# Gate and up projections of three FFNs as two by two block products: seven for eight

## The chip, the cores and the metric

The kernel runs on one core of one Trainium2 chip. The metric is device microseconds of one launch, the median of several runs. Profiles come from one profiled execution, which has a time of its own.

## The reference

A trunk of two decoder layers over 512 positions of width 1024, in float32. Each layer is a half FFN, a mixer, and a second half FFN, each added to x:

```
def swiglu_half(x, g, w_gate, w_up, w_down):
    h = rms_norm(x, g)
    return (jax.nn.silu(h @ w_gate) * (h @ w_up)) @ w_down
# x = x + 0.5 * swiglu_half(...)   four times: FFN 1 to 4; d_ff = 2816
```

Layer 0 mixes by MLA and dilated window attention, layer 1 by window attention with sinks and sparse attention. So the order is FFN 1, mixer 0, FFN 2, FFN 3, mixer 1, FFN 4.

## The kernel before, in words

x lies transposed on the chip: 8 tiles `x[d]` of 128 (width) x 512 (positions). TensorE multiplies in fp32r, and every operand is split in two: hi, its value cast to fp32r (ScalarE), and lo, the rest (VectorE, `tensor_tensor` subtract). A product is three matmuls: hi x hi, lo x hi, hi x lo (`TERMS`). `split` (L165 to L172) makes the pair; for weights it is one cast `whi<-raw` and one subtraction `wlo<-raw,whi` per tile of up to 1024 columns, three raw buffers deep.

An FFN (`ffn`, L262) runs in two halves of 11 features (a feature is 128 of the 2816 columns). For a feature, gate (bank `pg`) and up (`pu`) take 8 width tiles x 3 terms = 24 matmuls of 512 columns each, every one with its own weight load. `gated` (L295) scales both by the norm `rb` on VectorE, takes the silu on ScalarE, multiplies, and splits the result in ah and al. Then the half's down product follows: 8 blocks `py`, 33 matmuls each, and `x<-py,x` (L289).

The norm is put off: matmuls read x times the gain (`norm_tile`, L176: xh, xl of a d as soon as x[d] is done), and the sum of squares goes beside it (a square on ScalarE, an add on GpSimd, L195). `norm_wide` turns it into `rb` by a matmul with ones and by 9 VectorE operations of 512 columns (`rsqrt`). It is called in the first feature.

The Tile scheduler orders each engine's instructions by priority, which is the order of the code unless `high_priority` lifts them; each engine's queue is then served in order, and semaphores join them. Weight loads are DMAs on the SP queue. Buffers have tags with fixed counts (`UNITS`, `BANKS`): an allocation waits until the tile that had the buffer is done with.

## Time and profile before

| what | us |
|---|---|
| runs (3) | 2001.82, 2003.4, 2003.5; median 2003.4 |
| the profiled execution, its own time | 2003.07 |
| its span, first to last instruction | 2001.3 |
| TensorE busy | 1975.6 |
| VectorE, ScalarE, GpSimd busy | 1011.0, 754.2, 157.6 |

A row of the trace has the line, the engine, the operation, out<-in by the program's names, shapes and count; times are in us unless marked ns. PEld is the weight load, POOL is GpSimd, DVE VectorE, ACT ScalarE. A matmul's duration is longer than the step to the next, as they are pipelined: the step is read from two starts.

### The profile page before, as it was taken

To read this page: it belongs to the slowest core of one execution; us is meant where nothing else is said; L and a number is where in the kernel's file an instruction comes from. 1 tells how busy PE (TensorE), PEld (TensorE's weight loads), DVE (VectorE), ACT (ScalarE), POOL (GpSimd) and SP (SyncE) were. 2 spreads that over 40 slices of the span, in tenths; PEclk is the share of its full clock that TensorE was granted. 3 is DMA by queue.
4 is the path that set the end of the run, shared out by engine and by line. 5 is a ranking of instruction groups with operands and counts; after the bars stand their busy time and mean duration, and the time that the engine had idled before them with its cause. 6 is when DMAs were issued, how large, how long until landed. Compare 5 with 4: busy or idle time off the path is not lost.

```text
span 2001.3 us, 24703 instructions
## 1 busy us (share of the span) xinstructions
PE 1975.6 (99%) x9559; PEld 1628.5 (81%) x9559; DVE 1011.0 (51%) x1956; ACT 754.2 (38%) x1298; POOL 157.6 (8%) x219
## 2 busy tenths in 40 slices
PE   8999999999999999999999999999999999999999
PEld 6888888987967888888888888889987678888887
DVE  5443444477555644344454434445667765433442
ACT  4222333346555332232333223234267853322321
POOL 6100000112112000000100000001011220000000
PEclk9999999999999999999999999999999999999999
DMA  6523223421122222322332232244201132232323
GB/s 193 181 85 114 86 103 118 149 73 53 48 61 65 104 95 91 109 89 92 94 108 93 90 111 95 92 141 162 75 25 59 48 111 95 90 93 102 105 88 102
DMA packets 72854, 194.55 MB, mean 97 GB/s; under 512 B 9540, under 2 KB 16216, under 8 KB 72736
## 3 DMA queue, kind: packets, MB, share of 16 engines
q1 hardware_dynamic: 70752, 186.90, 28.3%
q0 software_dynamic: 1984, 6.06, 1.2%
q8 instruction: 75, 1.23, 0.2%
q14 instruction: 43, 0.35, 0.1%
HBM read 186.59 MB, written 12.35 MB: 99 GB/s over the span
## 4 chain that ended last, share of the span: by engine, by line
PE 95%; DVE 2%; ACT 1%; issue 1%; DMA 0%; POOL 0%; SPq 0%; DVEq 0%; ACTq 0%; POOLq 0%
PE py L162 27%; PE pg L162 24%; PE pu L162 24%; PE pz L404 10%; PE s L456 3%; PE po L497 2%; PE pt L434 2%; PE pqt L434 1%; ACT e L451 1%; PE pq L162 0%; PE ph L931 0%; DMA x<-in_xT 0%; ACT th L443 0%; DVE e L450 0%; PE pk L162 0%
## 5 line engine op out<-in xcount | busy, mean ns | idle before, releaser
L169 DVE TENSOR_TENSOR wlo<-raw,whi 128x1024 fp32r<-128x1024 f32 (+4 forms) x386 | 397.3, 1029 | 518.4 <-ACT whi L168 512.5
L168 ACT CAST whi<-raw 128x1024 fp32r<-128x1024 f32 (+4 forms) x386 | 345.4, 895 | 731.8 <-PE pu L162 298.7
L162 PE MATMUL pg<-xh,whi 128*128 128x512 f32 x704 | 276.0, 392 | 6.7 <-ACT xh L171 6.7
L162 PE MATMUL pg<-xl,whi 128*128 128x512 f32 x704 | 275.5, 391 | 1.9 <-DVE xl L172 1.9
L162 PE MATMUL pg<-xh,wlo 128*128 128x512 f32 x704 | 275.6, 391 | 0.0
L162 PE MATMUL pu<-xh,wlo 128*128 128x512 f32 x704 | 274.3, 390 | 0.0
L162 PE MATMUL pu<-xh,whi 128*128 128x512 f32 x704 | 274.0, 389 | 0.0
L162 PE MATMUL pu<-xl,whi 128*128 128x512 f32 x704 | 273.9, 389 | 0.0
L162 PE MATMUL py<-ah,whi 128*128 128x512 f32 x704 | 273.9, 389 | 0.0
L162 PE MATMUL py<-ah,wlo 128*128 128x512 f32 x704 | 273.9, 389 | 0.0
L162 PE MATMUL py<-al,whi 128*128 128x512 f32 x704 | 273.9, 389 | 0.0
L301 ACT ACTIVATE tg<-tg 128x512 f32<-128x512 f32 x88 | 55.6, 632 | 323.1 <-DVE tg L300 323.1
L162 PEld LDWEIGHTS pg<-xh,whi 128*128 128x128 f32 x704 | 132.5, 188 | 35.9 <-ACT xh L171 8.0
L162 PEld LDWEIGHTS pg<-xh,wlo 128*128 128x128 f32 x704 | 132.7, 188 | 35.1 <-DVE wlo L169 1.2
L162 PEld LDWEIGHTS pg<-xl,whi 128*128 128x128 f32 x704 | 132.5, 188 | 29.3 <-DVE xl L172 4.5
L162 PEld LDWEIGHTS pu<-xl,whi 128*128 128x128 f32 x704 | 132.1, 188 | 27.7 <-issue 0.2
L162 PEld LDWEIGHTS pu<-xh,wlo 128*128 128x128 f32 x704 | 132.1, 188 | 27.6 <-issue 0.2
L162 PEld LDWEIGHTS py<-ah,whi 128*128 128x128 f32 x704 | 132.1, 188 | 27.6
L162 PEld LDWEIGHTS py<-al,whi 128*128 128x128 f32 x704 | 132.1, 188 | 27.6
L162 PEld LDWEIGHTS pu<-xh,whi 128*128 128x128 f32 x704 | 132.2, 188 | 27.4
L162 PEld LDWEIGHTS py<-ah,wlo 128*128 128x128 f32 x704 | 132.1, 188 | 27.1
L300 DVE TENSOR_TENSOR tg<-pg,rb 128x512 f32<-128x512 f32 x88 | 60.8, 691 | 179.4 <-PE pg L162 179.3
(291 smaller groups left out, 2592.7 us busy)
## 6 DMA issues: line engine op xcount, KB each, us to landing
raw<-in_gu SPq DMA_DIRECT2D x174, 512.0 KB, 3.5
raw<-in_dn SPq DMA_DIRECT2D x64, 384.0 KB, 3.0
raw<-in_dn SPq DMA_DIRECT2D x64, 320.0 KB, 2.8
raw<-in_cd SPq DMA_DIRECT2D x14, 512.0 KB, 3.4
raw<-in_abqk SPq DMA_DIRECT2D x12, 512.0 KB, 3.8
xd<-x SPq DMA_DIRECT2D x16, 256.0 KB, 2.0
x<-xd SPq DMA_DIRECT2D x16, 256.0 KB, 4.0
raw<-in_abv SPq DMA_DIRECT2D x6, 512.0 KB, 3.6
```

The costliest lines, as they stand in the source:

```text
L162: self.nc.tensor.matmul(p, lhsT=w, rhs=x, start=n == 0, stop=n == len(terms) - 1)
L168: nc.scalar.copy(hi, src)
L169: nc.vector.tensor_tensor(lo, src, hi.bitcast(F32), OP.subtract)
L300: nc.vector.tensor_tensor(tg, ps[0], rb, OP.mult)
L301: nc.scalar.activation(tg, tg, AF.Silu)
L404: self.nc.tensor.matmul(ps[i], lhsT=sel(self.xg[k][b], i), rhs=wt[a][:, k - ks[0]], start=first, stop=k == KT - 1 and b == 1, skip_group_c ...
L434: self.turn = self.nc.tensor.transpose(p[:o[0], o[1]:o[1] + 128], s, self.identr if s.dtype == F32R else self.ident)
L451: nc.scalar.activation(s, s, AF.Exp, bias=st, scale=-1.0, accum_out=ss)
L456: self.nc.tensor.matmul(d, lhsT=a[:, q * 128:(q + 1) * 128], rhs=b[:, cols[0]:cols[1]], start=start and n == 0, stop=n == len(terms) - 1, ...
L497: self.nc.tensor.matmul(o, lhsT=v, rhs=t, start=first and k == 0, stop=last and k == len(heads[0]) - 1, skip_group_check=True)
```

## The change

FFN 2 to 4 use `ffn_combined`. Per feature, the 2 x 2 blocks of the weights are gate and up by lower and upper half of the width (a11, a12 gate; a21, a22 up); those of x are the width halves by the halves of the positions (256 columns). Seven products of 4 width tiles x 3 terms replace eight:

- `combine` loads a feature's weights as two raw tiles and makes four sums of 128 x 512 on GpSimd; `part` splits them (ScalarE, VectorE): 11 with s3, s1 with s2, 12 with 22, and s4.
- `norm_pair` makes the sums of x for tiles p and p+4 on GpSimd and VectorE, and splits them. The down and output products before such an FFN run their blocks in the order `PAIRED`.
- The products go to halves of three banks p, q, r. ScalarE copies p, q and r's first products out, VectorE and GpSimd put gate and up together (uu, tg, tu), and the scaling by rb is on GpSimd (tu) and VectorE (tg).
- `then` ties each of these instructions behind the last one on its engine: ACT, DVE and POOL run them in the order written. The splits for feature f+1 and the sums for f+2 stand between the steps of f, and the silu and splitting of f-1 too.
- Down runs after thirds of 8, 7 and 7 features instead of halves of 11.
- Buffers: raw four for three; z 17 and 4 pairs for 25; e and b one less. In mixer 0 the steps a20 and a11 change places. FFN 1 stays as it was, but that its last down product runs its blocks in the order `PAIRED`.

```diff
@@ -34,12 +34,16 @@
         "F3": (256, (0, 8), 1, 0, 127, 1),
         "F4": (512, (8, 16), 1, 0, 511, 1)}
-UNITS = {"x": 8, "xm": 16, "z": 25, "o": 8, "qk": 4, "e": 9, "t": 6, "h": 2, "b": 5}
+UNITS = {"x": 8, "xm": 16, "zz": 4, "z": 17, "o": 8, "qk": 4, "e": 8, "t": 6, "h": 2, "b": 4}
 BANKS = {"s": 2, "t": 2, "o": 1, "q": 1, "f": 2}
+RAWS = 4
 TERMS = ((0, 0), (1, 0), (0, 1))
-
-ORDER0 = """a10 !p0 a00 !h0 !h1 !p1 a20 a01 a11 a12 a02 !h2 s10 !s00 a21 s02 !h3 !s11 !s12 s01 !o0 !o1"""
+THIRDS = (0, 8, 15, 22)
+PAIRED = (0, 4, 1, 5, 2, 6, 3, 7)
+ORDER0 = """a10 !p0 a00 !h0 !h1 !p1 a11 a01 a20 a12 a02 !h2 s10 !s00 a21 s02 !h3 !s11 !s12 s01 !o0 !o1"""
 SCALE_F, SCALE_D, SCALE_T, SCALE_W = "vgvg", "gavv", "ggav", "avgv"
 SQUARE = "ggva"
...
-        return self.pu.tile([128, 512], dt, name=name, tag=tag, bufs=UNITS[tag])
+        return self.pu.tile([128, 1024 if tag == "zz" else 512], dt, name=name, tag=tag, bufs=UNITS[tag])
+    def doubled(self, name):
+        t = self.u("zz", name)
+        return [t[:, 0:512], t[:, 512:1024]]
     def ps(self, tag, name, dt=F32):
         return self.pp.tile([128, 512], dt, name=name, tag=tag, bufs=BANKS[tag])
...
@@ -121,7 +130,7 @@
     def load(self, src):
         a, b = src.shape[1:]
-        raw = self.pw.tile([128, a * b], F32, name="raw", tag="raw", bufs=3)
+        raw = self.pw.tile([128, a * b], F32, name="raw", tag="raw", bufs=RAWS)
         self.nc.sync.dma_start(raw, src.rearrange("p a b -> p (a b)"))
         return raw
...
@@ -180,9 +189,43 @@
             nc.sync.dma_start(self.xd[d], x)
         hi, lo = self.u("xm", "xh", F32R), self.u("xm", "xl", F32R)
         self.split(x, hi, lo, self.gn[:, j, d:d + 1])
-        self.xg.append((hi, lo))
+        self.xg.setdefault(d, (hi, lo))
         if squares:
             self.squares(d)
+    def norm_next(self, j, d, paired, spill=False):
+        if not paired:
+            self.norm_tile(j, d, spill)
+            return
+        self.squares(d)
+        if d >= 4:
+            self.norm_pair(j, d - 4)
+    def norm_pair(self, j, p):
+        nc = self.nc
+        n = 14 * p // 2
+        tags = (["xm"] * 16 + ["z"] * 12)[n:n + 7]
+        g = [self.u("t", "xg") for _ in range(2)]
+        for t, d in zip(g, (p, p + 4)):
+            nc.scalar.activation(t, self.x[d], AF.Copy, scale=self.gn[:, j, d:d + 1])
+        lo, hi = slice(0, 256), slice(256, 512)
+        c = [self.u("t", "xc") for _ in range(2)]
+        nc.gpsimd.tensor_tensor(c[0][:, lo], g[0][:, hi], g[0][:, lo], OP.subtract)
+        nc.vector.tensor_tensor(c[0][:, hi], g[1][:, hi], c[0][:, lo], OP.subtract)
+        nc.gpsimd.tensor_tensor(c[1][:, lo], g[1][:, hi], g[0][:, hi], OP.subtract)
+        nc.vector.tensor_tensor(c[1][:, hi], g[1][:, lo], c[0][:, hi], OP.subtract)
+        b = {}
+        for m, (t, names) in enumerate(((g[1], ("21", "22")), (c[0], ("t1", "t2")), (c[1], ("t3", "t4")))):
+            h, l = self.u(tags[2 * m], "xh", F32R), self.u(tags[2 * m + 1], "xl", F32R)
+            self.split(t, h, l)
+            for name, half in zip(names, (lo, hi)):
+                b[name] = h[:, half], l[:, half]
+        t = self.u(tags[6], "xh", F32R)
+        b["11"] = t[:, lo], t[:, hi]
+        self.split(g[0][:, lo], *b["11"])
+        self.xg.append(b)
     def squares(self, d):
         nc, x = self.nc, self.x[d]
...
@@ -263,8 +306,8 @@
         nc = self.nc
         gu, dn = self.A["gu"][li], self.A["dn"][li]
         xg = self.xg
-        self.xg = []
-        atags = ["o"] * 8 + ["e"] * 9 + ["b"] * 3 + ["qk"] * 2
+        self.xg = {}
+        atags = ["o"] * 8 + ["e"] * 8 + ["b"] * 3 + ["qk"] * 3
         for half in range(2):
             a = []
             for f in range(half * HF, (half + 1) * HF):
...
@@ -282,14 +325,144 @@
                 self.gated(a, ps, rb, atags)
                 if setup and f > 1:
                     next(setup, None)
-            for d in range(KT):
-                w = self.weights(dn[half, d], 6)
+            for d in PAIRED if half else range(KT):
+                w = self.weights(dn[d][:, half * HF:half * HF + HF], 6)
                 p = self.ps("f", "py")
                 self.mm3(p, [(w[f][i], a[f][j]) for f in range(HF) for i, j in TERMS])
                 nc.vector.scalar_tensor_tensor(self.x[d], p, 0.5, self.x[d], OP.mult, OP.add)
                 if half:
                     if nj is not None:
-                        self.norm_tile(nj, d, spill)
+                        self.norm_next(nj, d, False, spill)
+                    if out is not None:
+                        nc.sync.dma_start(out[:, d, :], self.x[d])
+    def then(self, eng, op, *args):
+        e = {"a": self.nc.scalar, "v": self.nc.vector, "g": self.nc.gpsimd}[eng]
+        with self.tc.issue_after(self.last[eng].ins) if eng in self.last else nullcontext():
+            self.last[eng] = getattr(e, op)(*args)
+    def parts_then(self, src, hi, lo):
+        self.then("a", "copy", hi, src)
+        self.then("v", "tensor_tensor", lo, src, hi.bitcast(F32), OP.subtract)
+    def combine(self, src):
+        r = [self.load(src[:, 4 * n:4 * n + 4]).rearrange("p (a b) -> p a b", a=4) for n in range(2)]
+        g, u = slice(0, 128), slice(128, 256)
+        a11, a21, a12, a22 = r[0][:, :, g], r[0][:, :, u], r[1][:, :, g], r[1][:, :, u]
+        s = self.u("zz", "ws").rearrange("p (a b) -> p a b", a=4)
+        v = self.u("h", "wv").rearrange("p (a b) -> p a b", a=4)
+        s1, s2 = s[:, :, g], s[:, :, u]
+        self.then("g", "tensor_tensor", s1, a21, a22, OP.add)
+        self.then("g", "tensor_tensor", a21, a11, a21, OP.subtract)
+        self.then("g", "tensor_tensor", s2, s1, a11, OP.subtract)
+        self.then("g", "tensor_tensor", v, a12, s2, OP.subtract)
+        return (("11", "s3"), r[0], None), (("s1", "s2"), s, "zz"), (("12", "22"), r[1], None), (("s4",), v, "qk")
+    def part(self, w, names, t, tag):
+        hl = [self.u(tag, "wc", F32R) for _ in range(2)] if tag else self.weight_parts(1024)
+        hl = [x.rearrange("p (a b) -> p a b", a=4) for x in hl]
+        self.parts_then(t, *hl)
+        for name, cs in zip(names, (slice(0, 128), slice(128, 256))):
+            w[name] = [x[:, :, cs] for x in hl]
+    def ffn_combined(self, li, nj, out=None, spill=False, paired=False):
+        nc = self.nc
+        gu, dn = self.A["gu"][li], self.A["dn"][li]
+        xg = self.xg
+        self.xg = [] if paired else {}
+        self.last = {}
+        atags = ["o"] * 8 + ["e"] * 8
+        lo, hi = slice(0, 256), slice(256, 512)
+        rb, then = None, self.then
+        def product(p, w, x, first, last, ks=range(4)):
+            for k in ks:
+                for n, (i, j) in enumerate(TERMS):
+                    nc.tensor.matmul(p, lhsT=w[i][:, k], rhs=xg[k][x][j], start=first and k == n == 0,
+                                     stop=last and (k, n) == (3, 2), skip_group_check=True)
+        def gate(part):
+            tg, tu = late
+            if part == 0:
+                then("a", "activation", tg, tg, AF.Silu)
+                then("v", "tensor_tensor", tu, tu, tg, OP.mult)
+            else:
+                n = 2 * len(a)
+                a.append((self.u(atags[n], "ah", F32R), self.u(atags[n + 1], "al", F32R)))
+                self.parts_then(tu, *a[-1])
+        c = {0: self.combine(gu[0])}
+        for f0, f1 in zip(THIRDS, THIRDS[1:]):
+            a, wn = [], {}
+            with self.tc.high_priority(offset=1000):
+                for t in c[f0]:
+                    self.part(wn, *t)
+                c[f0 + 1] = self.combine(gu[f0 + 1])
+            for f in range(f0, f1):
+                w, wn = wn, {}
+                p, q, r = self.ps("s", "pg"), self.ps("t", "pu"), self.ps("f", "pr")
+                ap, uu = self.u("b", "ap"), self.u("b", "uu")
+                tg, tu = self.u("t", "tg"), self.u("t", "tu")
+                early = [(p[:, lo], w["11"], "11", True, False), (q[:, lo], w["s3"], "t3", True, True),
+                         (r[:, lo], w["s1"], "t1", True, False)]
+                by = 1 if f < 2 else 4
+                for k in range(0, 4, by):
+                    for e in early:
+                        product(*e, range(k, k + by))
+                more = f < f1 - 1
+                with self.tc.high_priority(offset=2000):
+                    then("a", "copy", ap[:, lo], p[:, lo])
+                    then("a", "copy", tg[:, lo], q[:, lo])
+                    if more:
+                        self.part(wn, *c[f + 1][0])
+                    then("a", "copy", ap[:, hi], r[:, lo])
+                    if more:
+                        self.part(wn, *c[f + 1][3])
+                    if f > f0:
+                        gate(0)
+                product(p[:, lo], w["12"], "21", False, True)
+                product(q[:, lo], w["s2"], "t2", False, True)
+                with self.tc.high_priority(offset=2000):
+                    then("v", "tensor_tensor", uu[:, hi], q[:, lo], ap[:, lo], OP.add)
+                    then("g", "tensor_tensor", uu[:, lo], uu[:, hi], tg[:, lo], OP.subtract)
+                    then("g", "tensor_tensor", tu[:, hi], uu[:, hi], ap[:, hi], OP.add)
+                    if f > f0:
+                        gate(1)
+                    if more:
+                        self.part(wn, *c[f + 1][1])
+                        if f + 2 < NF:
+                            c[f + 2] = self.combine(gu[f + 2])
+                product(r[:, hi], w["22"], "t4", False, True)
+                product(r[:, lo], w["s4"], "22", False, True)
+                if rb is None:
+                    rb = self.norm_wide()
+                with self.tc.high_priority(offset=2000):
+                    if more:
+                        self.part(wn, *c[f + 1][2])
+                    then("v", "tensor_tensor", tu[:, lo], r[:, hi], uu[:, hi], OP.add)
+                    then("g", "tensor_tensor", tu, tu, rb, OP.mult)
+                    then("v", "tensor_tensor", tg[:, hi], r[:, lo], uu[:, lo], OP.add)
+                    then("v", "tensor_tensor", tg[:, hi], tg[:, hi], rb[:, hi], OP.mult)
+                    then("v", "tensor_tensor", tg[:, lo], p[:, lo], rb[:, lo], OP.mult)
+                    late = tg, tu
+                    if not more:
+                        gate(0)
+                        gate(1)
+            self.last = {}
+            for d in PAIRED:
+                wd = self.weights(dn[d][:, f0:f1], 8)
+                p = self.ps("f", "py")
+                self.mm3(p, [(wd[f][i], a[f][j]) for f in range(f1 - f0) for i, j in TERMS])
+                nc.vector.scalar_tensor_tensor(self.x[d], p, 0.5, self.x[d], OP.mult, OP.add)
+                if f1 == NF:
+                    if nj is not None:
+                        self.norm_next(nj, d, paired, spill)
                     if out is not None:
                         nc.sync.dma_start(out[:, d, :], self.x[d])
...
@@ -569,7 +742,7 @@
         self.xg = []
         nf = len(feats)
-        for d in range(KT):
+        for d in PAIRED if nj is not None else range(KT):
             w = self.weights(src[d], nf)
             p = self.ps("f", "py")
             self.mm3(p, [(w[f][a], feats[f][b]) for f in range(nf) for a, b in TERMS])
...
@@ -582,7 +755,7 @@
                         mybir.DependencyClass.NoSync, mybir.DependencyReason.SCHED_ONLY), reason="room")
             self.nc.vector.tensor_tensor(self.x[d], p, self.x[d], OP.add)
             if nj is not None:
-                self.norm_tile(nj, d)
+                self.norm_next(nj, d, True)
     def feature(self, o, tag):
         h, l = self.u(tag, "oh", F32R), self.u(tag, "ol", F32R)
...
@@ -1167,10 +1340,10 @@
         w0 = t.load_x()
         t.ffn(0, 1, setup=t.bias_build(), spill=True, w0=w0)
         t.mix0(2)
-        t.ffn(1, 3)
-        t.ffn(2, 4, spill=True)
+        t.ffn_combined(1, 3, paired=True)
+        t.ffn_combined(2, 4, spill=True)
         t.mix1(5)
-        t.ffn(3, None, out)
+        t.ffn_combined(3, None, out)
 def kernel(**inputs):
...
```

## Rows read from the trace of the kernel before

**Rows 1.** The page: engines, and the chain that ended last by engine

```profile
PE 1975.6 (99%) x9559; PEld 1628.5 (81%) x9559; DVE 1011.0 (51%) x1956; ACT 754.2 (38%) x1298; POOL 157.6 (8%) x219
...
PE 95%; DVE 2%; ACT 1%; issue 1%; DMA 0%; POOL 0%; SPq 0%; DVEq 0%; ACTq 0%; POOLq 0%
```

**Rows 2.** Windows: busy us (count) of PE, PEld, DVE, ACT, POOL; granted clock

```profile
833.30:953.20 119.90, 119.90 (x530) 98.69 (x529) 53.92 (x64) 36.13 (x43) 0.00 (x0) 1.00 0.27 93
...
1817.60:1937.50 119.90, 119.90 (x529) 98.69 (x528) 53.93 (x64) 36.13 (x43) 0.00 (x0) 1.00 0.27 93
```

**Rows 3.** Timeline of PE: a feature's first matmul, and the next feature's

```profile
898.69 0.39 PE L162 MATMUL pg<-xh,whi 128*128 128x512 f32 x1
...
909.59 0.39 PE L162 MATMUL pg<-xh,whi 128*128 128x512 f32 x1
```

**Rows 4.** Timeline of PE: first and last of 96 matmuls of 256 columns

```profile
548.87 0.28 PE L404 MATMUL pz<-whi,xh 128*128 128x256 f32 x1
...
560.27 0.28 PE L404 MATMUL pz<-whi,xl 128*128 128x256 f32 x1
```

**Rows 5.** Groups by shape, ACT: count | busy us, mean ns | idle

```profile
L168 ACT CAST whi<-raw 128x1024 fp32r<-128x1024 f32 x206 | 216.8, 1052 | 364.3 <-PE pu L162 272.4 <-PE pz L404 60.4 <-PE py L162 25.1
...
L301 ACT ACTIVATE tg<-tg 128x512 f32<-128x512 f32 x88 | 55.6, 632 | 323.1 <-DVE tg L300 323.1
...
L168 ACT CAST ah<-tu 128x512 fp32r<-128x512 f32 x88 | 54.7, 622 | 46.6 <-DVE tu L303 46.6
...
L842 ACT ACTIVATE zp<-pz 128x256 f32<-128x256 f32 x16 | 5.4, 388 | 1.8 <-PE pz L404 1.8
```

**Rows 6.** Groups by shape, DVE

```profile
L169 DVE TENSOR_TENSOR wlo<-raw,whi 128x1024 fp32r<-128x1024 f32 x206 | 252.1, 1224 | 296.2 <-ACT whi L168 295.9
...
L169 DVE TENSOR_TENSOR al<-tu,ah 128x512 fp32r<-128x512 f32 x88 | 60.2, 685 | 8.2 <-ACT ah L168 8.2
...
L169 DVE TENSOR_TENSOR wlo<-raw,whi 128x256 fp32r<-128x256 f32 x26 | 11.0, 422 | 16.8 <-ACT whi L168 16.5
```

**Rows 7.** Groups by shape, POOL

```profile
L195 POOL TENSOR_TENSOR sqa<-sqa,sqt 128x512 f32<-128x512 f32 x42 | 59.4, 1415 | 1073.1 <-ACT sqt L194 1066.3 <-DVE wlo L169 6.4
...
L480 POOL TENSOR_SCALAR e<-e,rs 128x512 f32<-128x512 f32 x24 | 18.9, 786 | 0.0
...
L558 POOL TENSOR_TENSOR e<-e,mx 128x512 f32<-128x512 f32 x8 | 8.4, 1053 | 48.2 <-DVE mx L556 46.4 <-PE py L162 1.6 <-PE pt L434 0.2
...
L795 POOL TENSOR_TENSOR rt<-qr,tab 128x256 f32<-128x256 f32 x2 | 1.5, 737 | 28.1 <-DVE ms L778 17.3 <-DVE rsm L219 10.7
```

**Rows 8.** Timeline of DVE and POOL before FFN 2: start, duration

```profile
652.66 0.74 DVE L172 SCALAR_TENSOR_TENSOR xl<-x,gn,xh 128x512 fp32r<-128x512 f32 x1
...
652.77 1.80 POOL L195 TENSOR_TENSOR sqa<-sqa,sqt 128x512 f32<-128x512 f32 x1 [1.64 <-ACT sqt L194]
...
653.33 0.69 DVE L583 TENSOR_TENSOR x<-py,x 128x512 f32<-128x512 f32 x1
...
654.24 1.42 DVE L169 TENSOR_TENSOR wlo<-raw,whi 128x1024 fp32r<-128x1024 f32 x1 [0.23 <-ACT whi L168]
...
655.50 1.30 POOL L195 TENSOR_TENSOR sqa<-sqa,sqt 128x512 f32<-128x512 f32 x1 [0.93 <-ACT sqt L194]
...
655.58 1.77 DVE L172 SCALAR_TENSOR_TENSOR xl<-x,gn,xh 128x512 fp32r<-128x512 f32 x1
```

**Rows 9.** Timeline of DVE and POOL in mixer 0

```profile
439.12 2.71 POOL L807 TENSOR_TENSOR lk<-lk,mr 128x256 f32<-128x256 f32 x4 [4.72 <-DVE mr L233]
...
439.28 0.83 DVE L807 TENSOR_TENSOR lq<-lq,mr 128x256 f32<-128x256 f32 x1
...
440.04 0.70 DVE L806 TENSOR_TENSOR lk<-kr,mr 128x128 f32<-128x128 f32 x1
...
442.03 0.28 DVE L806 TENSOR_TENSOR lk<-kr,mr 128x128 f32<-128x128 f32 x1
...
442.43 0.41 DVE L807 TENSOR_TENSOR lq<-lq,mr 128x256 f32<-128x256 f32 x1
```

More of the change, by code (lines that the diff above doesn't have):

```diff
@@ L310, in load_x @@
         nc = self.nc
-        self.x, self.xg = [], []
+        self.x, self.xg = [], {}
         self.xd = [self.pd.tile([128, T], F32, name="xd%d" % d, tag="xd%d" % d) for d in range(KT)]
@@ L315, in load_x @@
             if d % 4 == 0:
-                raw = self.pw.tile([128, 1024], F32, name="raw", tag="raw", bufs=3)
+                raw = self.pw.tile([128, 1024], F32, name="raw", tag="raw", bufs=RAWS)
                 parts = raw, *self.weight_parts(1024)
@@ L597, in mix0 @@
         zm = [self.u("z", "zm") for _ in range(4)]
-        self.perm = [self.u("z", "perm").rearrange("p (a t) -> p a t", a=4) for _ in range(2)]
+        self.perm = [t.rearrange("p (a t) -> p a t", a=4) for t in self.doubled("perm")]
         for n in range(2):
@@ L615, in values @@
             for k in gs:
-                zv[k] = [self.u("z", "zv") for _ in range(2)]
+                zv[k] = self.doubled("zv")
             def emit(i, p):
@@ L839, in part @@
         def part(n, scaled=False):
-            z = two([self.u("z", "zp") for _ in range(2)])
+            z = two(self.doubled("zp"))
             self.proj(A["cd%d" % n], nat,
@@ L1081, in pack_ffn @@
     u = up.reshape(KT, 128, NF, 128).transpose(2, 1, 0, 3)
-    d = down.reshape(2, HF, 128, KT, 128).transpose(0, 3, 2, 1, 4)
+    d = down.reshape(NF, 128, KT, 128).transpose(2, 1, 0, 3)
     return np.concatenate([g, u], -1), d
```

## The prediction

> **What bounds the kernel now.** I read the page's engine shares first: TensorE is busy 1975.6 of 2001.3 us, VectorE 51%, ScalarE 38%, GpSimd 8% [rows 1]. The chain that ended last is 95% PE [rows 1]. So a microsecond taken from TensorE's stream is a microsecond of the kernel, until another engine takes over the pace; the work that this change puts on three lightly used engines is what has to be weighed. Next the windows: a half of gate and up (11 features) lasts 119.9 us in FFN 2 and 119.9 in FFN 4, with PE busy throughout, at a granted clock of 1.00, and POOL idle [rows 2]. The timeline gives the step: the first gate matmul of a feature starts at 898.69, that of the next at 909.59, so 10.90 us for 48 matmuls of 512 columns, 0.227 each [rows 3]. The halves of [rows 2] are 11 such steps, so I take it for all 66.
>
> The profiled execution took 2003.07 us with a span of 2001.3; the median of the runs is 2003.4. I sum against 2003.1.
>
> **What TensorE saves.** After, a feature is 7 products x 4 blocks x 3 terms = 84 matmuls of 256 columns, each with its own weight load, for 48 of 512. The nearest row is a projection of 256 columns with a new weight for every matmul: 96 of them start between 548.87 and 560.27, 11.40 / 95 = 0.120 us each [rows 4]. So 84 x 0.120 = 10.08 us for 10.90: not an eighth but 7.5%, since some 13 ns a matmul don't shrink with the columns. Over 66 features 54 us can be gained, no more. The weight load is no bound: a load lasts 98.69 / 529 = 187 ns [rows 2], yet loads at every matmul went at 0.120. The Trainium skill ("TensorE: Matmul & The Clock Gate", Back-to-back issue gap) gives N / 2.4 + 2.5 ns for an isolated matmul, 109 ns here; by that a feature would be an estimated 9.2 us. The trace disagrees (120 ns), and I keep its value. Down keeps its 528 matmuls.
>
> **What the other engines get**, per feature in mid-third. *ACT*: casts of 3 x 1024 and one 512 column tile, three PSUM copies of 256, silu, ah: 3 x 1.05 + 0.62 + 3 x 0.39 + 0.63 + 0.62 = 6.2 us [rows 5]. Under 10.08: alone it costs nothing. *DVE*: differences lo of 3 x 1024 and 512, the product tu x tg, al, five ops of 256: 3 x 1.22 + 3 x 0.69 + 5 x 0.42 = 7.8 us [rows 6]. Also under. *POOL*: four weight sums of 512, tu x rb of 512, two ops of 256. Add of two separate tiles of 512: 1415 ns mean, 1290 where it met little (below); 256 elements: about 0.74 [rows 7], a group that had DVE beside it. So 5 x 1.29 + 2 x 0.74 = 7.9 us. Each engine by itself fits, and by engine shares alone the change wins.
>
> **What speaks against it: VectorE and GpSimd exclude each other.** [Rows 8] read in order of ends: the DVE scalar_tensor_tensor of 652.66 ends at 653.40, the POOL add that started at 652.77 ends at 654.57: 1.17 later. DVE's wlo of 654.24 then ends at 655.66, 1.09 after POOL. POOL's add of 655.50 ends at 656.80, 1.14 after DVE; and the DVE op of 655.58 ends at 657.35, 0.55 after POOL, and shows 1.77 us where it takes 0.74 free. Nothing of one ran beside the other but its start (0.14 of POOL's 1.29, 0.13 of DVE's 1.22). In [rows 9] four POOL multiplies run in 2.71 us while DVE's ops of 128 and 256 elements take 0.70 and 0.83, and 0.28 and 0.41 once POOL is done: one DVE op between two of POOL. The exception: x<-py,x, which reads PSUM, took its 0.69 us in the middle of a POOL add [rows 8]. So DVE ops with two SBUF inputs and POOL ops queue for one thing, and their held times add. The Trainium skill ("SBUF — State Buffer", Who interferes with whom) says the same, an exclusive lock for a VectorE instruction with two SBUF inputs against a GpSimd one that reads SBUF, but for the whole instruction; by that the holds would be the full durations, third rival's sum.
>
> Held times of one feature: POOL 5 x 1.15 + 2 x 0.60 = 6.95 (0.74 - 0.14 = 0.60); DVE, without the four ops that read PSUM, 3 x 1.09 (wlo) + 3 x 0.55 (lo of s4, tu x tg, al) + 0.28 (tg x rb, half of 0.55) = 5.20. Together 12.15 us, above TensorE's 10.08 and above the 10.90 of now. Change-overs add: in [rows 9] 4 x 0.46 (half of the 0.9 below) + 0.28 + 2 x 0.15 + 0.14 = 2.56 of holds took 2.71. The set orders add waits with the lock free: behind POOL's tu x rb, DVE's tu x tg, al and both lo of the next weights are queued in order, and PE's third product waits for the lo of s1. I take 12.5; the ends are 12.15 and 14.1 (nothing overlaps). Below, no row shows a strided weight sum on POOL; the cheapest two-input row is 1053 ns (one input broadcast) [rows 7], 0.9 held: 10.6, second rival.
>
> Not every feature pays: at a third's start two features' sums are already done under the down product, so I let the first two of each third run at 10.08. 16 x 12.5 + 6 x 10.08 = 260.5 us per FFN, against 22 x 10.90 = 239.8: **+20.7**.
>
> **The rest, per FFN.**
> - rb (norm_wide) is 9 ops of 512 with two SBUF inputs in the first features: 9 x 0.55 = 5 us more in the lock; now DVE's idle time hides them. **+5** (0 to 7).
> - Ends of thirds: down's last feature waits for tg, rb, silu, tu x tg, ah, al: 3 x 0.42 + 0.63 + 0.69 + 0.62 + 0.69 = 3.9 us, under a cover of 6 or 7 features x 3 x 0.227 = 4.1 to 4.8. Hidden if POOL is on time; here tu x rb comes late. **+5** for two (0 to 8).
> - norm_pair before each FFN: after the last x come a square, a scaled copy, POOL's 0.74, a cast, a lo: 0.62 + 0.62 + 0.74 + 0.62 + 0.69 = 3.3 us, plus about 2 of other casts in the two queues; cover from the interleaved start is 3 blocks x 9 x 0.120 = 3.2. **+2.5** (0 to 4).
> - Three thirds for two halves: down's weight casts are 1024 or 896 columns for 768 and 640, the same total, covered by 5 us a block. A fourth raw buffer, two of them held over the down product: loads of 3.5 us against 10 us. Zero (-1 to +2).
>
> Sum 20.7 + 12.5 = 33 us, three times: 100. The mixers (a11 and a20 exchanged, one e and one b unit less, z in pairs) and FFN 1 (block order): PE's idle time in the whole span is 26 us, so -6 to +8; I take none. **2003.1 + 100 = 2103, forecast 2100.**
>
> **Rivals.**
> *1, the other side: TensorE keeps the pace.* If POOL's strided sums hold so little that the lock sum stays under 10.08, 54.1 us are gained, less 3 x 2.5 for norm_pair and 3 x 2.5 for rb: 2003.1 - 39 = 1964. It decides at (10.08 - 5.20 - 0.92) / 5 = 0.79 us held per POOL op of 512 (0.46 for one of 256). For it: each engine is under 10.08 by itself. Against: only a one-input op was that short (786 ns) [rows 7].
> *2, short holds.* POOL at 0.90 and 0.46: 5.42 + 5.20 = 10.62, with change-overs 11.0: 16 x 11.0 + 60.5 = 236.5, -3.3, plus 11: +8 per FFN, 2027. For it: a POOL group is that short; against: it broadcasts one operand, and the sums read two full ones.
> *3, full durations add.* 5 x 1.29 + 2 x 0.74 + 3 x 1.22 + 3 x 0.69 + 0.42 = 14.1: 16 x 14.1 + 60.5 = 286.1, +46 + 12.5 per FFN, 2179. Against it: the hidden starts of [rows 8].
>
> **Chances.** Forecast 0.62 (own range 2050 to 2145: 12.15 to 13.2 a feature, the extras at their ends), rival 1 0.19, rival 2 0.13 (2000 to 2050), rival 3 0.05, the rest 0.01. About 0.2%, 4 us, is what a measurement of this kernel tells from no change. Faster is rival 1 and the lowest end of rival 2: 0.21; within 0.2%: 0.04; slower: 0.75. The range 1975 to 2145 leaves out most of rival 1 and rival 3, some 0.19.
>
> **What would show it.** Right: in mid-third the step from one feature to the next is over 12 us, PE waits some 2 us in it, mostly for wlo; wlo of 1024 shows well over 1.22 us and POOL's sums over 1.29; the first two features of a third run near 10.1; PE's busy time is down by up to 54 us while the span grows. Wrong: a steady step of 10.1 us without PE waits (rival 1), POOL sums near 1.04 (rival 2), a pitch far from 0.120 (the TensorE step), or wlo at 1.22 beside a running POOL op (the lock).

## The result: 2192.2 us, 9.4% slower, 92 us above the forecast

The median of 4 runs is 2192.16 us (2186.05 to 2197.31), that of the kernel before, run beside it, 2002.8: ratio 1.0945 [1.0914, 1.0975]. The forecast was 2100, the range ended at 2145. The sign was right; the size was not. The profiled span went from 2001.3 to 2188.2, +186.9 us.

The page of the changed kernel, against [rows 1] (engines: busy us, share, instructions; then the chain that ended last, by engine):

```profile
PE 2016.8 (92%) x11935; PEld 1752.2 (80%) x11935; DVE 1413.5 (65%) x2334; ACT 921.1 (42%) x1652; POOL 901.9 (41%) x705
...
PE 54%; POOL 23%; DVE 12%; issue 6%; ACT 4%; DMA 0%; SPq 0%; POOLq 0%; DVEq 0%; ACTq 0%
```

No engine but TensorE is busy more than 65%, yet the chain runs through GpSimd and VectorE for 35% of the span. TensorE's busy time rose by 41 us although it multiplies less, and its mean granted clock fell from 0.998 to 0.966.

**A step in mid-third.** One ACT copy ap<-pr stands in each feature, so the distance of two is the step that [rows 3] gave as 10.90:

```profile
884.94 0.36 ACT L343 COPY ap<-pr 128x256 f32<-128x256 f32 x1
...
897.85 0.37 ACT L343 COPY ap<-pr 128x256 f32<-128x256 f32 x1
```

12.91 us; over the 7 features of FFN 2's second third the steps are 10.39, 12.72, 12.88, 12.88, 12.91, 10.20. By TensorE's own starts the first two features of this third take 10.07 and 10.08, the next 11.1, then some 12.9 each. TensorE's timeline in one such step (start, duration; in brackets the idle time before and who ended it):

```profile
880.65 0.47 PE L386 MATMUL pr<-xh,wc 128*128 128x256 f32 x1 [1.45 <-DVE wc L343]
...
883.06 0.41 PE L386 MATMUL pg<-xh,whi 128*128 128x256 f32 x1
883.27 0.41 PE L386 MATMUL pg<-xh,wlo 128*128 128x256 f32 x1
...
884.40 0.28 PE L386 MATMUL pg<-xh,wlo 128*128 128x256 f32 x1
884.52 0.28 PE L386 MATMUL pg<-xl,whi 128*128 128x256 f32 x1
...
893.54 0.38 PE L386 MATMUL pr<-xh,wc 128*128 128x256 f32 x1 [1.06 <-DVE wc L343]
...
895.77 0.39 PE L386 MATMUL pg<-xh,wlo 128*128 128x256 f32 x1 [0.54 <-DVE wlo L343]
```

The pitch is 0.12, as [rows 4] had it, and 0.21 for a while after the longer wait. What TensorE waits for is the lo half of the combined weights (wc) and of the raw ones (wlo), both from VectorE. The table of its waits (us in total, times, longest):

```profile
PE pr L386 <- DVE wc L343: 53.2, 42, 1.5
PE pg L386 <- DVE wlo L343: 32.1, 39, 6.7
PE py L171 <- ACT ah L343: 24.8, 9, 4.0
```

Why VectorE is late stands in the groups by shape (count | busy us, mean ns | idle before), against [rows 6, 7]:

```profile
L343 DVE TENSOR_TENSOR wlo<-raw,whi 128x1024 fp32r<-128x1024 f32 x132 | 232.8, 1764 | 43.2 <-ACT whi L343 43.2
...
L343 POOL TENSOR_TENSOR ws<-raw 128x512 f32<-128x512 f32 x66 | 140.1, 2123 | 226.1 <-DMA raw<-in_gu 226.1
...
L343 POOL TENSOR_TENSOR ws<-ws,raw 128x512 f32<-128x512 f32 x66 | 102.6, 1555 | 0.0
...
L343 DVE TENSOR_TENSOR uu<-pu,ap 128x256 f32<-128x256 f32 x66 | 27.2, 412 | 6.0 <-PE pu L386 6.0
```

wlo of 1024 shows 1764 ns for 1224, a GpSimd sum 1555 to 2123 for the 1290 it takes alone; uu, which reads PSUM, isn't lengthened (412; an operation of 256 columns took 422 in [rows 6]). The timeline shows how, read in order of ends as [rows 8] was:

```profile
891.20 1.20 POOL L343 TENSOR_TENSOR tu<-uu,ap 128x256 f32<-128x256 f32 x1
...
891.72 1.76 DVE L343 TENSOR_TENSOR wc<-ws,wc 128x1024 fp32r<-128x1024 f32 x1
...
892.37 2.27 POOL L343 TENSOR_TENSOR ws<-raw 128x512 f32<-128x512 f32 x1
...
893.41 2.31 DVE L343 TENSOR_TENSOR wlo<-raw,whi 128x1024 fp32r<-128x1024 f32 x1
...
894.71 2.16 POOL L343 TENSOR_TENSOR raw<-raw 128x512 f32<-128x512 f32 x1
```

Ends: 892.40 (GpSimd), 893.48 (VectorE, 1.08 later), 894.64 (GpSimd, 1.16), 895.72 (VectorE, 1.08), 896.87 (GpSimd, 1.15). The two engines take strict turns, and a turn lasts what the prediction had from three rows.

**A third and its down product.** Windows (us, busy us (count) of PE, PEld, DVE, ACT, POOL, granted clock), against [rows 2]; FFN 2's start, two stretches of 11 and 10 us; then its first down product from the long wait on; then its second third:

```profile
662.70:673.90 11.20, 4.49 (x21) 4.15 (x21) 10.17 (x8) 4.15 (x7) 10.42 (x9) 0.64 0.13 47
673.90:684.00 10.10, 6.45 (x21) 4.54 (x20) 8.73 (x14) 4.48 (x10) 3.54 (x3) 0.50 0.15 52
...
790.00:831.50 41.50, 41.27 (x171) 33.97 (x172) 16.94 (x16) 8.50 (x9) 4.57 (x3) 0.93 0.28 85
831.50:914.40 82.90, 75.18 (x589) 72.73 (x589) 62.48 (x68) 36.38 (x59) 68.21 (x44) 0.98 0.28 88
```

At the start TensorE issues 21 matmuls in 11 us, with VectorE and GpSimd both busy over 90%, and then 21 in 10 us at a granted clock of 0.50, the lower level (1.2 GHz). In the first block of the down product, before the third's last feature, it stands for 4.02 us:

```profile
785.82 0.39 PE L171 MATMUL py<-al,whi 128*128 128x512 f32 x1
790.23 0.80 PE L171 MATMUL py<-ah,whi 128*128 128x512 f32 x1 [4.02 <-ACT ah L343]
790.82 0.63 PE L171 MATMUL py<-ah,wlo 128*128 128x512 f32 x1
791.25 0.63 PE L171 MATMUL py<-ah,whi 128*128 128x512 f32 x1
...
795.73 0.40 PE L171 MATMUL py<-ah,wlo 128*128 128x512 f32 x1
795.97 0.39 PE L171 MATMUL py<-al,whi 128*128 128x512 f32 x1
```

After that wait matmuls of 512 start 0.43 apart for 5 us, then 0.24 and 0.23 apart again. The ah it waited for is that of the third's last feature, and that stands behind the one before, whose product on VectorE waited for GpSimd's tu x rb, queued behind four weight sums (DVE, then POOL):

```profile
781.57 0.69 DVE L343 TENSOR_TENSOR tu<-tu,tg 128x512 f32<-128x512 f32 x1 [2.44 <-POOL tu L343]
...
780.25 1.29 POOL L343 TENSOR_TENSOR tu<-tu,rb 128x512 f32<-128x512 f32 x1
```

Behind it on VectorE come that feature's al and the lo part of a down weight, and only then the last feature's tu:

```profile
783.96 1.75 DVE L178 TENSOR_TENSOR wlo<-raw,whi 128x1024 fp32r<-128x1024 f32 x1
785.63 0.41 DVE L343 TENSOR_TENSOR tu<-pr,uu 128x256 f32<-128x256 f32 x1
```

**Where the 186.9 us are**, from the starts of TensorE's stages in the two traces. FFN 2's first feature lasts from its first matmul to that of the second, 11.34 us before and 28.03 after (22.7 in FFN 3, 26.6 in FFN 4):

```profile
652.91 0.39 PE L162 MATMUL pg<-xh,whi 128*128 128x512 f32 x1
...
664.25 0.40 PE L162 MATMUL pg<-xh,whi 128*128 128x512 f32 x1
```

```profile
662.74 0.28 PE L386 MATMUL pg<-xh,whi 128*128 128x256 f32 x1
...
690.77 0.28 PE L386 MATMUL pg<-xh,whi 128*128 128x256 f32 x1
```

| part, FFN 2 to 4 together | before | after | more |
|---|---|---|---|
| stretches ahead of FFN 2 and of FFN 4 | | | +18 |
| first feature of each FFN | 3 x 11.3 | 3 x 25.8 | +43 |
| other features of first thirds (7 steps) | 3 x 76.5 | 3 x 90.8 | +43 |
| gate and up of thirds 2 and 3 | 6 x 76.3 | 6 x 82.5 | +37 |
| down products | 3 x 119.7 | 3 x 134.8 | +45 |

FFN 1 adds the last 0.5.

### The profile page after: what moved, and what is told of

Same layout as the page of the kernel before. It is cut to its first block, busy times and chain, and to the rows that moved or that the text cites. A ratio compares the mean times of both kernels' runs of the same rounds, so it can differ in the third digit from the quotient of the medians.

```text
span 2188.2 us, 30955 instructions
## 1 busy us (share of the span) xinstructions
PE 2016.8 (92%) x11935; PEld 1752.2 (80%) x11935; DVE 1413.5 (65%) x2334; ACT 921.1 (42%) x1652; POOL 901.9 (41%) x705
## 4 chain that ended last, share of the span: by engine, by line
PE 54%; POOL 23%; DVE 12%; issue 6%; ACT 4%; DMA 0%; SPq 0%; POOLq 0%; DVEq 0%; ACTq 0%
PE py L171 22%; PE pz L577 9%; POOL ws L343 9%; PE pu L171 5%; PE pg L171 5%; POOL wv L343 5%; POOL raw L343 5%; POOL tu L343 3%; PE s L629 2%; DVE tu L343 2%; PE po L670 2%; PE pt L607 2%; DVE wc L343 2%; PE pg L386 1%; ACT wc L343 1%
## 5 line engine op out<-in xcount | busy, mean ns | idle before, releaser
L177 ACT CAST whi<-raw 128x1024 fp32r<-128x1024 f32 (+5 forms) x230 | 201.8, 877 | 440.2 <-PE py L171 245.2
L178 DVE TENSOR_TENSOR wlo<-raw,whi 128x1024 fp32r<-128x1024 f32 (+5 forms) x230 | 244.9, 1065 | 200.0 <-ACT whi L177 198.0
L171 PE MATMUL py<-ah,whi 128*128 128x512 f32 x704 | 280.9, 399 | 26.9 <-ACT ah L343 24.8
L386 PE MATMUL pr<-xh,wc 128*128 128x256 f32 x1056 | 221.4, 299 | 66.7 <-DVE wc L343 53.2
L343 DVE TENSOR_TENSOR wlo<-raw,whi 128x1024 fp32r<-128x1024 f32 x132 | 232.8, 1764 | 43.2 <-ACT whi L343 43.2
L386 PEld LDWEIGHTS pr<-xh,wc 128*128 128x128 f32 x1056 | 174.4, 199 | 83.6 <-DVE wc L343 63.0
L343 POOL TENSOR_TENSOR ws<-raw 128x512 f32<-128x512 f32 x66 | 140.1, 2123 | 226.1 <-DMA raw<-in_gu 226.1
L386 PE MATMUL pg<-xh,whi 128*128 128x256 f32 x792 | 193.9, 296 | 5.1 <-DVE tg L343 4.1
L386 PE MATMUL pg<-xh,wlo 128*128 128x256 f32 x528 | 161.4, 306 | 32.4 <-DVE wlo L343 32.1
L386 PE MATMUL pr<-xl,wc 128*128 128x256 f32 x528 | 154.8, 293 | 2.7 <-DVE xl L178 2.7
L577 PE MATMUL pz<-whi,xh 128*128 128x256 f32 (+3 forms) x448 | 149.1, 333 | 0.0
L577 PE MATMUL pz<-whi,xl 128*128 128x256 f32 (+3 forms) x448 | 146.9, 328 | 0.0
```

Source lines behind the costliest of these rows:

```text
L171: self.nc.tensor.matmul(p, lhsT=w, rhs=x, start=n == 0, stop=n == len(terms) - 1)
L177: nc.scalar.copy(hi, src)
L178: nc.vector.tensor_tensor(lo, src, hi.bitcast(F32), OP.subtract)
L343: self.last[eng] = getattr(e, op)(*args)
L386: nc.tensor.matmul(p, lhsT=w[i][:, k], rhs=xg[k][x][j], start=first and k == n == 0, stop=last and (k, n) == (3, 2), skip_group_check=True)
L577: self.nc.tensor.matmul(ps[i], lhsT=sel(self.xg[k][b], i), rhs=wt[a][:, k - ks[0]], start=first, stop=k == KT - 1 and b == 1, skip_group_c ...
```

## Experiments

The theory: the steady features go by the shared turns of VectorE and GpSimd (some 80 us), FFN starts and down products add the rest (some 106 us). Rivals: the set order makes the waits; the sums cost by themselves, not by sharing; GpSimd's length alone is the bound. "Before" is always the kernel before, run beside.

**1. GpSimd nearly as busy, but nothing read for the sums.** Each weight sum becomes two fills of the same tile, so the combined weights are constants.

```
-        self.then("g", "tensor_tensor", s1, a21, a22, OP.add)
...
+        for t in (s1, a21, s2, v):
+            for _ in range(2):
+                self.then("g", "memset", t, 0.03)
```

> The four weight sums on GpSimd are left out: each is replaced by two memsets of the same tile (8 x about 0.53 us, so GpSimd's queue is held about as long as by 4 x 1.29, but its instructions read no SBUF). The sums' values are constants, so the products with s1 to s4 are not those of the reference. Sharing theory (DVE with two SBUF inputs and GpSimd reads exclude each other): held times 5.20 + 2.35 = 7.6 us lie under TensorE's 10.08, the step of a feature in mid-third falls from 12.89 to 10.1 to 10.4 us, wlo of 1024 from 1.76 back to 1.22, the first feature of an FFN from 28 to about 15; in all 1960 to 2010 us. Rival (GpSimd's queue as such, or the order that the queues are tied to): GpSimd is as busy and in the same place, the step stays over 12.3, 2150 us or more.

2009.29 us, ratio 1.002 [1.0001, 1.004]: all but 7 us of the 189 are gone. That is a balance: thirds 2 and 3 now run 34 us under the kernel before, while the stretches ahead, the first thirds and the down products are still 41 over. The first feature takes 22.9 us in FFN 2, where about 15 was expected. The fills take GpSimd 1.1 us a pair and VectorE's wlo beside them is undisturbed (DVE, then POOL):

```profile
839.46 1.21 DVE L343 TENSOR_TENSOR wlo<-raw,whi 128x1024 fp32r<-128x1024 f32 x1
...
839.44 1.11 POOL L343 MEMSET raw<- 128x512 f32 x2
```

Steps are 10.08 us, TensorE's own 84 x 0.120, and a third of 7 features takes 70.55. What delayed TensorE in steady features is that GpSimd's sums read SBUF, as VectorE's two-input operations do, not their order or their number. This agrees with the Trainium skill ("SBUF — State Buffer", Who interferes with whom), where a GpSimd instruction that only writes doesn't contend. A pair of fills is a little shorter than a sum by itself (1.11 and 1.29 us), and fills wait for no weights; so the next run asks what one sum costs, and experiment 6 keeps every sum.

**2. One sum of four taken out** (the last, for s4, by two fills).

```
-        self.then("g", "tensor_tensor", v, a12, s2, OP.subtract)
+        self.then("g", "memset", v, 0.03)
+        self.then("g", "memset", v, 0.03)
```

> One of the four weight sums on GpSimd (that of s4) is left out and replaced by two memsets. If held times add, the step of a feature is their sum, 12.15 - 1.15 = 11.0, plus the 0.74 by which the change stands above its sum: 11.6 to 11.8 us, 2080 to 2125 in all. If the lock is not what sets the step (or only beyond some load): 12.9 or 10.1.

2120.14 us (one run), step 11.73. From 12.89 that is 1.16 less for one sum whose held time was put at 1.15. So here one sum costs the step its turn, to 0.01:

```profile
857.24 0.37 ACT L343 COPY ap<-pr 128x256 f32<-128x256 f32 x1
...
868.98 0.36 ACT L343 COPY ap<-pr 128x256 f32<-128x256 f32 x1
```

The Trainium skill ("SBUF — State Buffer", SBUF: two separate sides) has the shared ports held for the whole instruction, which would be 1.29 here; the runs say 1.16.

**3. The four sums on VectorE instead.**

```
-        self.then("g", "tensor_tensor", s1, a21, a22, OP.add)
+        self.then("v", "tensor_tensor", s1, a21, a22, OP.add)
...
```

> The four weight sums run on VectorE instead of GpSimd, at the same place of the order; nothing is left out. Sharing theory: GpSimd holds 2.35 us a feature (tu x rb and two of 256), VectorE 5.20 + 4 x 0.55 = 7.4, together 9.75, just under TensorE's 10.08; VectorE's own queue is about 9.4. Step 10.1 to 10.6 us, in all 1985 to 2040. Rival (VectorE's own load is what stretched the step, GpSimd only waits for it): by durations VectorE now has 7.8 + 4 x 0.69 = 10.6 us a feature, the step is 11.5 or more, in all over 2080.

2109.26 us, ratio 1.0527 [1.0496, 1.0557]; step 11.97. The expected step was missed, and the rival's (11.5 or more, over 2080 in all) was met. Two groups of this run (as above), and its second third of FFN 2:

```profile
L343 DVE TENSOR_TENSOR ws<-raw 128x512 f32<-128x512 f32 x66 | 50.8, 770 | 0.0
...
L343 DVE TENSOR_TENSOR tg<-tg,rb 128x256 f32<-128x256 f32 x66 | 81.1, 1229 | 2.1
...
817.64:896.51 78.87, 71.80 (x589) 70.78 (x588) 75.10 (x99) 38.78 (x61) 19.96 (x18) 1.00 0.29 91
```

A sum on VectorE is short, but VectorE is now at its own end (75.10 of 78.87 us), and GpSimd's remaining three operations still take turns with it: tg x rb, 0.43 us where GpSimd is idle (experiment 6), shows 1.23 behind GpSimd's tu x rb. 5.20 of two-input work, 4 x 0.35 from PSUM (0.41 less the overlap of two starts), 4 x 0.69 of sums and GpSimd's 1.15 + 2 x 0.60 make 11.7. I had taken VectorE's queue (9.4) and the sum of the turns (9.75) as two bounds side by side; the queue is in order and has no room, so GpSimd's turns come on top of it. Whether VectorE's load alone would do it is left to experiment 6.

**4. The set order taken away.**

```
-        with self.tc.issue_after(self.last[eng].ins) if eng in self.last else nullcontext():
-            self.last[eng] = getattr(e, op)(*args)
+        getattr(e, op)(*args)
```

> The instructions of ACT, DVE and POOL are no longer tied behind each other; the scheduler orders them. Sharing theory: the held times still sum to 12.15 us, no order brings the step under that; 12.2 or more in mid-third, in all 2150 to 2250. Rival (the set order makes the waits): the step falls under 11.5, in all under 2100.

2308.39 us, ratio 1.152 [1.1487, 1.1554], steps some 15.2: worse than expected. The order isn't the cause; it saves 116 us.

**5. All of the change but the FFNs** (buffers, mixers, FFN 1's block order).

```
-        t.ffn_combined(1, 3, paired=True)
+        t.ffn(1, 3)
...
```

> All of the change but the FFNs: FFN 2 to 4 run as before (48 matmuls of 512 columns, norm tile by tile), with the new buffers, four raw tiles, the new order of mixer 0 and of the blocks. If the 18 us that the two stretches from mixer start to FFN start got longer come from the pair sums and the early weight sums on GpSimd: 2003 us, within 6. Rival (buffers and orders make the mixers slower): 2015 to 2022.

2010.18 us, ratio 1.004 [1.0013, 1.0068]; the medians differ by 7.6 us, between what was expected (2003 within 6) and the rival's 2015; the profiled spans differ by 4.4 us (2005.7 and 2001.3): FFN 2 starts 2.2 later, mixer 1 takes 2.0 longer, the FFNs are as before. So 4 of the 18 us ahead of FFN 2 and FFN 4 are these, and 14 are left for the pair sums and the first combined weights.

**6. Nothing of it on GpSimd.** Sums and subtractions on VectorE; the factor rb, which cost an operation per feature, is applied where down is added to x.

```
-        self.then("g", "tensor_tensor", s1, a21, a22, OP.add)
+        self.then("v", "tensor_tensor", s1, a21, a22, OP.add)
...
-                    then("g", "tensor_tensor", tu, tu, rb, OP.mult)
...
+                nc.vector.scalar_tensor_tensor(y, p, 0.5, rb, OP.mult, OP.mult)
+                nc.vector.tensor_tensor(self.x[d], y, self.x[d], OP.add)
```

> Nothing is left out, but GpSimd has no work in FFN 2 to 4 except the eight adds of squares: the weight sums, the two evictions of 256 columns and the pair sums of x are on VectorE, and the scaling of tu by rb is put off to the eviction of down (x += 0.5 rb y, one more VectorE operation a block). Sharing theory, as the sum that fitted the kernel with the sums on VectorE (VectorE's queue 9.4 + GpSimd's 2.35 held = 11.75, measured 11.97): with no GpSimd the queue is 3 x 1.14 + 7 x 0.61 + 7 x 0.34 = 10.07 us, equal to TensorE's 10.08; step 10.1 to 10.7, in all 1995 to 2045. Rival (VectorE's load alone set the 11.97): this kernel gives VectorE more work, step 11.9 or more, in all 2090 or more.

2024.97 us, ratio 1.0104 [1.0089, 1.012]. Thirds 2 and 3 run at TensorE's pace (70.55 for 76.3), here the second of FFN 2:

```profile
803.60:874.15 70.55, 70.55 (x589) 70.55 (x588) 68.47 (x112) 38.43 (x61) 0.00 (x0) 1.00 0.31 101
```

VectorE has 112 instructions in it where experiment 3 has 99, and the step is 10.08 for 11.97: so VectorE's load alone did not set the 11.97. Every sum is made here, and in these thirds they cost TensorE nothing (in first thirds the steady steps are 10.45). The downs of FFN 2 are 43.6, 38.2 and 39.0, together 1.2 over the old 119.7 (in experiment 1, where tu x rb stayed, 44.6, 39.4 and 40.9, 5.2 over, so most of the down waits, too, come from the sums' turns). What is left is the start: FFN 2 begins at 665.98 (652.91 before) and first thirds take 94.0, 102.1 and 94.5 for 87.9.

**7 and 8. The start: is it the priority of the first weights?** They are lifted ahead of the pair sums; here not, once without GpSimd's work and once in the change itself.

```
-            with self.tc.high_priority(offset=1000):
+            with self.tc.high_priority(offset=1000 if f0 else 0):
```

> The kernel before this one, and the weight parts of an FFN's first feature and the sums of its second no longer lifted ahead (priority offset 1000) of the last output or down blocks. If the first feature's 28 us come from those operations standing in VectorE's queue ahead of the last x and its pair sums, some 5 to 10 us an FFN go: 1965 to 2020, 15 to 30 below the kernel before. Rival (the chain from the last x through the pair sums is what takes the time, whatever stands before): the same within 6 us.

> The change with the one edit at the start of an FFN: first parts and second sums not lifted ahead. Queue theory: the first feature of each FFN 8 to 15 us shorter, in all 2140 to 2170. Rival (the chain from the last x): 2180 to 2195.

2023.13 us (1.0095 [1.0077, 1.0113]), 2 us under experiment 6, and 2204.29 (1.0999 [1.0953, 1.1046]), 12 above the change (and 9 above the rival's range): that theory fell. A window of the former, just ahead of FFN 2's first product at 665.40, shows why:

```profile
655.00:665.00 10.00, 2.26 (x10) 1.50 (x8) 10.00 (x18) 5.65 (x10) 3.24 (x3) 0.73 0.16 52
```

VectorE works all 10 us of 10. There is more to do there than TensorE has work to cover, in either of the two orders tried.

**9. Pair sums of x made late.** As experiment 6, but the first third of each FFN goes the old way on tiles normed one by one, and the pair sums are made beside its products and its down; 14 features of 22 are combined.

```
+            if f0 == 0:
+                for f in range(f1):
+                    w = self.weights(gu[f], 4)
...
+                    if f == 4:
+                        pairs = [self.norm_pair(j, 0)]
...
+                    if 0 < d < 4:
+                        pairs.append(self.norm_pair(j, d))
```

> The kernel without GpSimd (all sums on VectorE, rb at down's eviction), and in each of FFN 2 to 4 the first third runs as before the change (48 matmuls of 512, tiles normed one by one); the pair sums of x are made during that third and its down product, and only the other 14 features run as seven products. Nothing is left out. If the dear start (output blocks before an FFN 10 us longer, first feature 12 to 20) comes from the pair sums and the first weights crowding VectorE at the one moment when TensorE needs x: it is gone, and an FFN takes 360.1 - 14 x 0.82 = 348.6 us; with the 4 us that the buffers cost: 1965 to 1985, faster than both kernels. Rival (seven-product features are dear at any start, for instance by their first weights): thirds begin with a stall again and the time is over 2000.

**1979.94 us, ratio 0.9872 [0.9848, 0.9896]**: faster than both kernels. Its page and windows (first third, down, second third of FFN 2):

```profile
PE 1948.0 (98%) x11071; PEld 1675.7 (85%) x11071; DVE 1314.5 (66%) x2562; ACT 889.7 (45%) x1556; POOL 158.9 (8%) x219
```

```profile
652.00:742.00 90.00, 90.00 (x397) 73.94 (x396) 57.88 (x76) 35.29 (x46) 5.07 (x4) 1.00 0.34 105
742.00:786.00 44.00, 44.00 (x195) 36.43 (x195) 28.25 (x44) 20.66 (x29) 0.00 (x0) 1.00 0.31 96
786.00:857.00 71.00, 71.00 (x583) 70.54 (x582) 67.51 (x109) 36.90 (x59) 0.00 (x0) 1.00 0.33 101
```

In these windows TensorE has no gap and the full clock; in the second third VectorE is busy 95% with 109 instructions. The start's cost is gone with the pair sums' place: the first third takes 87.83 (87.86 before), FFN 2 starts at 657.17 (652.91 before, 665.98 in experiment 6).

**10. The same, with GpSimd's work as in the change.**

```
-        self.then("v", "tensor_tensor", s1, a21, a22, OP.add)
+        self.then("g", "tensor_tensor", s1, a21, a22, OP.add)
...
+                    then("g", "tensor_tensor", tu, tu, rb, OP.mult)
...
```

> The same late pair sums, but the weight sums, the two evictions, tu x rb and the pair subtractions on GpSimd as in the change. Sharing theory: the start is as cheap as before the change, thirds 2 and 3 keep their 82 to 83 us and their down waits, as nothing there is different: per FFN 87.6 + 43.6 + 82.9 + 45 + 82.1 + 39.5 = 381, in all 2060 to 2080. Rival (the slow thirds come out of the late start): 70 to 76 us a third, under 2030.

2078.02 us, ratio 1.0363 [1.0331, 1.0396]: first third 88.76, steps 12.9 again, thirds 2 and 3 82.86 and 83.55, downs 44.0 and 45.5 where experiment 9 has 43.5 and 39.3. Against experiment 9, GpSimd's part costs 98 us with 14 combined features.

## Why the prediction was wrong

*TensorE's step: right.* 84 x 0.120 = 10.08 us was the floor in thirds 2 and 3 of experiments 1, 6 and 9, to the hundredth.

*Turns of VectorE and GpSimd: right, in kind and size.* Held 12.15, taken 12.5, measured 12.9 (0.74 above the held sum, not 0.35; 0.62 of it stands where GpSimd's uu waits for VectorE's uu, which reads PSUM: GpSimd's ends at 891.25, 1.22 after VectorE's last turn, for a hold of 0.60); 1.08 and 1.15 us a turn were measured against 1.09 and 1.15 taken, and experiments 1, 2 and 6 show the cause. Features and rb together were to cost 25.7 an FFN, 77 in all; they cost 43 + 37 = 80. The closeness is partly luck: 13 features of an FFN ran at some 12.9, not 16 at 12.5, and the step with rb in it took 16.81. The cheap first two features came (10.07 and 10.08) in thirds 2 and 3, not in the first.

*Buffers and mixers: right.* 4.4 us by the spans and 7.6 by the medians, inside the -6 to +8.

*"Ends of thirds +5 (0 to 8)": failed, 15 an FFN, 45 in all.* The cover was set against a chain of free durations, "hidden if POOL is on time". It wasn't, for the same turns that lengthened the step: VectorE's product waited 2.44 us for tu x rb, TensorE 4.02 in the end. I had the lateness in words and not in the bound. The last feature's chain, from 785.63 to the end of ah at 790.18, took 4.55 us for the 3.9 of the sum; the 4.06 us before it, from 781.57, are VectorE's queue ahead of it. And the wait is paid twice: the 12 matmuls from 790.23 took 5.27 us for 12 x 0.227 = 2.72. The nine waits of the table above make 24.8 of the 45. The slower pitch adds some 15: 14 behind the six waits of 3.2 to 4.0 us, 0.7 behind the three of 1.25. Most of the rest is three waits of 0.7 us for tg and the first matmuls after waits. Without GpSimd's share (experiment 6) 1.2 us are left in FFN 2.

*"norm_pair before each FFN +2.5 (0 to 4)": failed, and by most.* 7.5 us were to stand for what measured 43 + 14 = 57. I followed the chain of the last x alone (3.3 us, and 2 of other casts). The trace shows that the last x itself is late (DVE, then PE):

```profile
667.40 0.68 DVE L756 TENSOR_TENSOR x<-py,x 128x512 f32<-128x512 f32 x1
...
669.61 2.30 DVE L343 TENSOR_TENSOR wc<-ws,wc 128x1024 fp32r<-128x1024 f32 x1
...
676.38 0.68 DVE L756 TENSOR_TENSOR x<-py,x 128x512 f32<-128x512 f32 x1
```

```profile
662.51 0.40 PE L171 MATMUL py<-ol,whi 128*128 128x512 f32 x1
...
669.74 0.58 PE L386 MATMUL pg<-xh,wlo 128*128 128x256 f32 x1 [6.71 <-DVE wlo L343]
```

TensorE ended its last block at 662.9; VectorE added it to x at 676.38, since its queue is in order and ten operations stood ahead of it from 663.7 on: pair sums, lo parts, combined weights. They took 12.7 us where, by durations without GpSimd beside them, they need about 7, the rest being GpSimd's turns. The right sum was the whole queue of VectorE from the last blocks on, not the chain behind x. Experiment 9 shows it from the other side: moved under the old first third, the same pair sums cost next to nothing, with GpSimd's part in them (88.76, experiment 10) or without (87.83), for 87.86. How much of the 57 us is queue, how much turns and how much lower clock was not separated. Experiment 1 bounds a part: with fills for the weight sums the first feature still takes 21.7 us on average (25.8 in the change, 11.3 before) and the two stretches ahead are 10 us longer (18), so some 20 us go with the reads of these sums. Experiment 6, with the adds of squares alone on GpSimd and the sums in VectorE's queue, still starts FFN 2 13.1 us late and pays 6 to 14 in each first third.

*PE's busy time "down by up to 54 us": wrong sign.* The sum had no term for the lower clock after a wait. It isn't all of the rise: a matmul ahead of a wait counts with its whole 0.28, not with the pitch of 0.12. FFN 2's second third shows 75.18 us busy for 588 x 0.120 = 70.6, at a granted clock of 0.98 over 82.9 us; over the whole span the two parts were not separated.

*The range.* The upper ends of the two failed terms, 12 an FFN, were 36 in all; the two measured 57 + 45 = 102. The own range and its 2145 rested on them. Rival 3 (2179) came near the time by another way than the one it names: full durations would have made the step 14.1, and it was 12.9.

## What to carry to other kernels

When two engines are to share work, write down for each instruction whether it reads SBUF twice on VectorE or at all on GpSimd, and add these turns into one sum; each engine's own busy share (65% and 41% here) did not show it. At every place where the phase changes, sum the whole in-order queue that stands ahead of the instruction the next phase needs, not the chain behind its input, and add what the lower clock costs after a wait. A saving on TensorE pays where the added work has a phase with room: with the change's work kept off GpSimd, 14 features with late pair sums gained 1.3% (experiment 9) and 22 with pair sums at the start lost 1.0% (experiment 6); with GpSimd's turns the same two lost 3.6% and 9.4%.

## Not expected of the hardware

- After 4.02 us without a matmul the next eleven of 512 columns started 0.43 us apart, then 0.23; at FFN 2's start ten us ran at a granted clock of 0.50, while TensorE was getting its operands piecemeal.
- A GpSimd fill of 512 elements per partition takes some 0.55 us (two in 1.11) and leaves VectorE's two-input operations untouched (1.21 us beside it).
- VectorE does a weight sum of 512 in 0.73 to 0.77 us (means of experiment 3), GpSimd an operation of that size in 1.29 alone; in the sums above each weight sum costs 0.55 to 0.69 on VectorE and 1.16 on GpSimd, so handing work to the idler engine made the sum larger.
